# Summing squares in bursts of four tiles, and passing sums of head outputs through DRAM, in a two-layer decoder step

## The chip, the core and the metric

One core of a Trainium2 chip runs the whole program. The metric is the device time of one execution in microseconds, the median of three runs. TensorE (PE) does the matmuls, VectorE (DVE) and ScalarE (ACT) the elementwise work, GpSimd (POOL) a few additions, and SyncE (SP) issues the DMAs, in order.

## The reference, cut to what matters

Two trunk layers run over 512 prompt tokens and 64 sample tokens (8 sequences of 8). In a layer:

```python
h = rmsnorm(x, pre_g)
proj = h @ w_in                                # 2048 -> 6144 columns
u, gp, q, k, v, gr = jnp.split(proj, SPLITS, axis=-1)
pool_y = pool_mixer(u, ...) * silu(gp)         # four groups of 256 channels
ret_y = head_rmsnorm(retention(q, k, v, ...)) * silu(gr)   # four heads of 256 channels
mix = concatenate([pool_y, ret_y]) @ w_out     # 2048 -> 2048
x = x + rmsnorm(mix, post_g)
ple = rmsnorm(p @ w_ple, ple_g)                # per-layer embedding, 256 -> 2048
gate = sigmoid(x @ w_ple_gate + b)
x = x + gate * ple
```

An rmsnorm needs, per token, the sum of the squares of all 2048 channels.

## The kernel before, in words

Activations lie with channels on the 128 partitions and the 576 tokens along the row, in tiles of 128x576 float32. A matmul takes half a row, 288 columns. To keep precision each operand is split into a high and a low part (`split`, L88: ScalarE copies the high part, L90, VectorE subtracts, L91), and a product is three matmuls (L116 to L118, L136, L226).

The large projections `w_in` (first half of its inputs), `w_out` and the gate's first half go through `unit` (L234), a scheme of seven block products in place of eight. It needs, for each pair of activation tiles x1, x2, the blocks themselves and four sums of them: T1 = b12 - b11, T2 = b22 - T1, T3 = b22 - b12, T4 = b21 - T2. `sums_of_blocks` (L186) takes them with four VectorE subtractions (L194 to L197) and splits the results.

A layer runs in this order:

- `in_first` and `in_phase`: the input projection. In `in_phase` the columns of the second half are computed head by head (`head`, L560): q, k, v, retention, state, norm, silu gate. At its end each head multiplies its two output tiles by the gate (L653) and writes them to `m_dram` (L654).
- The pooling groups (`pool_group`, L656), in the order 3, 2, 1, 0. After each group one pair of head outputs is loaded back from `m_dram` into tiles of the tag `x` (L717) and made into operands for the output projection (L711): splits and the four subtractions, into tiles of the tag `part`.
- `out_phase`: the output projection (16 units, L733), with the pooling outputs loaded and made into operands between units (L738). The squares of its results are summed on VectorE into `ssm` (L326), but for the last two tiles (L748). `rsqrt` (L294) then sums over the partitions on TensorE: `token_sums` (L292) multiplies each quarter of a row with a 128x32 matrix of ones, into 32 partitions of an accumulator of the tag `po` (2 buffers). The reciprocal root is some dozen small VectorE instructions (L300 to L306) in one scratch tile of the tag `tmp`, spread back over all partitions by L310 and L311.
- The embedding, L751 to L770: 16 tiles, each of 12 matmuls (L136) into two accumulators of the tag `acc` (4 buffers). ScalarE squares both halves into a tile of the tag `u` (L316) and copies them to a tile of the tag `part` (L768), which goes to DRAM (L770). `token_sums` sums the square into one accumulator over all 16 tiles (L769).
- The gate: the residual is formed (L778, L781) and split, the b12 blocks into tiles of the tag `u` (`plain="u"`, L817), the projection is run, and each tile is gated and added (L789 on).

Nothing orders the engines by hand but a few lines: `after_all` makes an instruction wait for given others, and `order` puts VectorE and ScalarE instructions behind the last one of a unit. All else is set by a planner that walks the program with costs of its own, takes ready instructions by their place in the program, and gives a tile one of its tag's buffers when its first writer is placed. A tag has a fixed number of buffers (L44): `tmp` 4, `part` 4, `x` 4, `u` 6, `g` 2.

Of the kernel before, what the change touches and what calls it, by code (L numbers as in the profile page):

```python
# [10 lines left out]
AF = mybir.ActivationFunctionType  # L11
ALU = mybir.AluOpType
# [3 lines left out]
L = 2  # L16
KT = 16
# [4 lines left out]
HN = NT // 2  # L22
QN = NT // 4
# [10 lines left out]
def half(ap, h):  # L34
    return ap[:, h * HN:(h + 1) * HN]
# [3 lines left out]
def decoder_kernel(ctx: ExitStack, tc: tile.TileContext, a, decay8):  # L39
    nc = tc.nc  # L40
# [5 lines left out]
    def buf(tag, shape=(P, NT), dt=F32):  # L46
        return sb.tile(list(shape), dt, tag=tag, name=tag, bufs=BUFS.get(tag, 1))
# [13 lines left out]
    def tmp():  # L61
        return buf("tmp")

    def load_const(name, shape):
        t = sb.tile(shape, F32, name="c_" + name)
        nc.sync.dma_start(out=t, in_=a[name])
        return t

    ones = sb.tile([P, 32], F32, name="ones")
# [10 lines left out]
    def dram(name, n=KT):  # L80
        return [tc.dram_tile([P, NT], F32, name=f"{name}{i}") for i in range(n)]

    x_dram, m_dram = dram("x"), [dram(f"m{l}") for l in range(L)]
    ple_dram = [dram(f"ple{l}") for l in range(L)]
    gate_dram = [dram(f"gate{l}") for l in range(L)]
    proj_dram = [dram(f"proj{l}", 48) for l in range(L)]

    def split(hi, lo, src, scale=None):  # L88
# [34 lines left out]
    def mix_tile():  # L123
        return ps.tile([P, 512], F32, tag="po", name="po", bufs=2)
# [17 lines left out]
    def operand_set():  # L142
        return {n: [] for n in ("b11", "b12", "t1", "t2", "t3", "t4", "b21", "b22", "src")}

    def order(ops):
        stack = ExitStack()
        for at in ("tail", "tail_act"):
            if at in ops:
                stack.enter_context(tc.issue_after(ops[at].ins))
        return stack  # L150
# [32 lines left out]
            ops["src"].append((x1[j], x2, new[j]))  # L183
        return ops

    def sums_of_blocks(ops, pairs=range(4), tag="u", engines=None):  # L186
        for j in pairs:
            x1, x2, new = ops["src"][j]
            b11, b12 = x1[:, :HN], x1[:, HN:]
            b21, b22 = x2[:, :HN], x2[:, HN:]  # L190
            eng = engines[j] if engines else nc.vector
            t12, t34 = (buf(tag) for _ in range(2))
            with order(ops):
                eng.tensor_tensor(out=t12[:, :HN], in0=b12, in1=b11, op=ALU.subtract)  # L194
                eng.tensor_tensor(out=t12[:, HN:], in0=b22, in1=t12[:, :HN], op=ALU.subtract)
                eng.tensor_tensor(out=t34[:, :HN], in0=b22, in1=b12, op=ALU.subtract)
                last = eng.tensor_tensor(out=t34[:, HN:], in0=b21, in1=t12[:, HN:], op=ALU.subtract)  # L197
            if eng is nc.vector:
                ops["tail"] = last
            for src, n1, n2 in ((t12, "t1", "t2"), (t34, "t3", "t4")):  # L200
                hi, lo = next(new)((P, NT)), next(new)((P, NT))
                split(hi, lo, src)
                ops[n1].append((hi[:, :HN], lo[:, :HN]))
                ops[n2].append((hi[:, HN:], lo[:, HN:]))
        return ops

    def operands(xs, pairs=range(4), ops=None, tag="u", slots=own_slots):
        ops = operand_set() if ops is None else ops
        for j in pairs:
            blocks(xs, [j], ops, slots)  # L210
            sums_of_blocks(ops, [j], tag)
        return ops

    def plain_unit(raw, ops, d0, d1):
# [75 lines left out]
    def token_sums(sums, src, start, stop):  # L290
        for q in range(4):
            nc.tensor.matmul(sums[32 * q:32 * q + 32], ones, src[:, q * QN:(q + 1) * QN], start=start, stop=stop)  # L292

    def rsqrt(out, srcs, n, sums=None):  # L294
        if sums is None:
            sums = mix_tile()[:, :QN]
            for i, src in enumerate(srcs):
                token_sums(sums, src, i == 0, i == len(srcs) - 1)
        v, t, r = (w[:, i * QN:(i + 1) * QN] for w in (tmp(),) for i in range(3))
        nc.vector.tensor_scalar(v, sums, 1.0 / n, EPS, op0=ALU.mult, op1=ALU.add)  # L300
        nc.vector.tensor_scalar(r.bitcast(I32), v.bitcast(I32), 1, None, op0=ALU.logical_shift_right)
        nc.vector.tensor_scalar(r.bitcast(I32), r.bitcast(I32), -1.0, float(0x5F3759DF), op0=ALU.mult, op1=ALU.add)
        for _ in range(3):
            nc.vector.scalar_tensor_tensor(out=t, in0=r, scalar=-0.5, in1=r, op0=ALU.mult, op1=ALU.mult)
            nc.vector.tensor_tensor(out=t, in0=t, in1=v, op=ALU.mult)
            nc.vector.scalar_tensor_tensor(out=r, in0=t, scalar=1.5, in1=r, op0=ALU.add, op1=ALU.mult)  # L306
        for h in range(2):
            rows = mix_tile()[:, :HN]
            for q in (2 * h, 2 * h + 1):
                nc.tensor.matmul(rows[:, (q % 2) * QN:(q % 2 + 1) * QN], pick[:, q], r, start=True, stop=True)  # L310
            nc.scalar.copy(half(out, h), rows)  # L311

    def square(out, src):
        if isinstance(src, list):
            for h in range(2):
                nc.scalar.activation(half(out, h), src[h], AF.Square)  # L316
        else:
            nc.scalar.activation(out, src, AF.Square)

# [11 lines left out]
    def load_tables():  # L331
# [6 lines left out]
        consts["kdec_s"] = load_const("kdec_s", [P, NH, NS])  # L338
        consts["mask_s"] = load_const("mask_s", [P, NH, 64])
        consts["invcnt"] = load_const("invcnt", [P, 4, 16])  # L340

    def after_all(ins, others):
        for other in others:
            tc.add_manual_dep(
                ins.ins, other.ins.name, mybir.DependencyInfo(mybir.DependencyClass.Sync, mybir.DependencyReason.DATA),
                reason="one burst",
            )

    def retention_state(l, h, s0_ring, qrep, kst, vst, po_s):
        for bg in range(2):  # L350
# [28 lines left out]
    pairs = []  # L379
# [89 lines left out]
    def in_phase(l, raws, r2, rB, cos, sin):  # L469
# [90 lines left out]
        def head(h):  # L560
# [3 lines left out]
            q = rotary(8 + h)  # L564
# [8 lines left out]
            k = rotary(12 + h)  # L573
# [33 lines left out]
            o = [rot_ring.tile() for _ in range(2)]  # L607
# [26 lines left out]
            sq, sq2 = tmp(), tmp()  # L634
# [17 lines left out]
            for i, g in enumerate(silu_gates(20 + h)):  # L652
                nc.vector.tensor_tensor(out=o[i], in0=o[i], in1=g, op=ALU.mult)  # L653
                nc.sync.dma_start(out=m_dram[l][8 + 2 * h + i], in_=o[i])  # L654

        def pool_group(g):  # L656
            w = WINDOWS[g]
# [50 lines left out]
        out_ops = operand_set()  # L708
        for j, g in enumerate(groups):
            pool_group(g)  # L710
            operands(mix_loader(l, 8), [j], out_ops, tag="part")  # L711
        return out_ops

    def mix_loader(l, first):
        def xs(k):
            t = buf("x")
            nc.sync.dma_start(out=t, in_=m_dram[l][first + k])  # L717
            return t
        return xs

    def out_phase(l, raws, ops_out):
# [3 lines left out]
        ops = {0: ops_out, 1: operand_set()}  # L725

        def out_step(n, g, p):
            cts = (2 * p, 2 * p + 1)
            fetch(l, raws, keys[n:n + 2])
            if g == 0:  # L730
                for ct in cts:
                    mo[ct] = slot(28 + ct)
            yield from unit(raws.pop(keys[n]), ops[g], mo[cts[0]], mo[cts[1]], g == 0, nc.gpsimd)  # L733
            fetch(l, raws, keys[n + 2:n + 3])
            if g == 0 and 1 <= p < 5:
                j = p - 1
                with order(ops[0]):
                    operands(mix_loader(l, 0), [j], ops[1], tag="d", slots=spare_slots if j < 2 else early_slots)  # L738
            if g:
                for ct in cts:  # L740
                    if ct < KT - 2:
                        square_into(ssm, mo[ct], ct == 0)
# [3 lines left out]
        last = [tmp() for _ in range(2)]  # L746
# [5 lines left out]
        for k in range(2):  # L752
            t = buf("x")
# [2 lines left out]
            split(hi, lo, t)  # L756
            pp.append((hi, lo))
        sums = mix_tile()[:, :QN]
        for c8 in range(2):
            raw = load_weights(a["w_ple"][l, :, c8 * 8:(c8 + 1) * 8].rearrange("p c k n -> p (c k) n"))  # L760
            w = split_weights(raw, 0, 16)
            for c in range(8):
                ct = c8 * 8 + c
                acc = gemm(w[2 * c:2 * c + 2], pp)
                t, sq = buf("part"), buf("u")
                square(sq, acc)
                for i in range(2):
                    nc.scalar.copy(half(t, i), acc[i])  # L768
                token_sums(sums, sq, ct == 0, ct == KT - 1)  # L769
                nc.sync.dma_start(out=ple_dram[l][ct], in_=t)  # L770

        def residual(first):
            def xs(k):
# [67 lines left out]
        x2, g2 = residual(8), []  # L841
# [7 lines left out]
        for p in range(8):  # L849
            raw = raws.pop(("gate2", p))  # L850
            for c in range(2):
                ct = 2 * p + c
                t = buf("part")
# [14 lines left out]
    ops = None  # L868
    for l in range(L):
        state = in_first(l, raws, ops)  # L870
        ops = in_phase(l, raws, *state)
        ops = out_phase(l, raws, ops)
# [93 lines left out]
```

## Time and profile before

| | |
|---|---|
| median of 3 runs | 2209.13 us (2203.75 to 2210.25) |
| profiled execution | 2208.09 us, span 2206.3 us |
| TensorE | busy 2179.7 us (99%) |
| VectorE | busy 1724.1 us (78%) |
| ScalarE | busy 1059.0 us (48%) |
| DMA | 361.98 MB, mean 164 GB/s |
| granted TensorE clock | 0.999 of full speed |

"Busy" is the time in which at least one instruction of the engine ran; matmuls overlap, and their ends are modelled, so for TensorE the distance from one start to the next says more than a duration. Times in rows are microseconds from the start of the span.

### The profile page before, as it was taken

Reading aid. Unit: us, or ns where it says so; the run is one execution under the profiler, and the core shown is the slowest. Engines: PE = TensorE matmul, PEld = TensorE weight load, DVE = VectorE, ACT = ScalarE, POOL = GpSimd, SP = SyncE. Lnnn points to the kernel's source line nnn. Section 1 sums busy time; section 2 is a strip of 40 time slices with the busy share of each in tenths; the row PEclk is TensorE's granted clock in tenths of the full one; section 3 lists DMA queues with packets and bytes.
Section 4 is the critical chain, followed back from the end, with each engine's and each line's share of the span. In section 5 each row is a group of like instructions: output and inputs, shape, how many; then the busy total and the mean of one; then the engine's idle time right before and its main releaser. Section 6 shows DMA issues by size and latency. Waiting matters only on the chain.

```text
span 2206.3 us, 42552 instructions
## 1 busy us (share of the span) xinstructions
PE 2179.7 (99%) x16692; PEld 2138.2 (97%) x16692; DVE 1724.1 (78%) x3186; ACT 1059.0 (48%) x2097; POOL 89.5 (4%) x65
## 2 busy tenths in 40 slices
PE   8999999999999999999999999999999999999998
PEld 8999999999999999899999999999999999998998
DVE  8788766767689998888877786666676899988865
ACT  5465433444334555655455554433343345566532
POOL 2000000000000110000110000000000011100000
PEclk9999999999999999999999999999999999999999
DMA  6454455546453434556644444455554543345554
GB/s 227 146 195 166 155 169 159 174 160 186 152 177 127 136 118 136 196 171 219 201 161 152 166 156 152 161 178 173 159 171 152 171 147 123 112 144 192 175 197 151
DMA packets 138729, 361.98 MB, mean 164 GB/s; under 512 B 14496, under 2 KB 52896, under 8 KB 117664
## 3 DMA queue, kind: packets, MB, share of 16 engines
q1 hardware_dynamic: 138528, 359.26, 49.3%
q8 instruction: 131, 2.15, 0.4%
q14 instruction: 70, 0.57, 0.1%
HBM read 273.17 MB, written 86.04 MB: 163 GB/s over the span
## 4 chain that ended last, share of the span: by engine, by line
PE 87%; DVE 5%; DMA 5%; issue 2%; ACT 1%; SPq 0%; POOL 0%; DVEq 0%; ACTq 0%; POOLq 0%
PE acc L136 32%; PE acc L118 12%; PE acc L117 12%; PE acc L116 12%; PE acc L226 4%; DMA x<-ple 3%; PE pb L116 3%; PE pb L117 3%; PE pb L118 3%; PE po L292 1%; PE po L136 1%; DVE wl L91 1%; DVE x L801 1%; PE po L359 1%; PE pb L375 1%
## 5 line engine op out<-in xcount | busy, mean ns | idle before, releaser
L136 PE MATMUL acc<-m,wh 128*128 128x288 f32 x3584 | 657.0, 297 | 4.0 <-DVE part L484 4.0
L90 ACT CAST wh<-raw 128x512 fp32r<-128x512 f32 x567 | 350.3, 619 | 530.3 <-PE acc L136 288.1
L117 PE MATMUL acc<-m,wh 128*128 128x288 f32 x1944 | 572.3, 295 | 0.0
L116 PE MATMUL acc<-m,wh 128*128 128x288 f32 x1944 | 570.4, 295 | 0.8 <-ACT m L249 0.8
L118 PE MATMUL acc<-m,wl 128*128 128x288 f32 x1944 | 566.3, 295 | 1.2 <-DVE wl L91 1.2
L136 PEld LDWEIGHTS acc<-m,wh 128*128 128x128 f32 x3584 | 534.7, 189 | 11.7 <-issue 8.4
L91 DVE TENSOR_TENSOR wl<-raw,wh 128x512 fp32r<-128x512 f32 x567 | 395.7, 700 | 130.1 <-ACT wh L90 122.7
L136 PE MATMUL acc<-m,wl 128*128 128x288 f32 x1792 | 396.9, 296 | 0.0
L116 PEld LDWEIGHTS acc<-m,wh 128*128 128x128 f32 x1944 | 364.3, 188 | 2.0 <-ACT m L249 1.5
L117 PEld LDWEIGHTS acc<-m,wh 128*128 128x128 f32 x1944 | 364.8, 188 | 0.0
L118 PEld LDWEIGHTS acc<-m,wl 128*128 128x128 f32 x1944 | 362.3, 188 | 2.1 <-DVE wl L91 2.1
L90 ACT CAST wh<-S 128x512 fp32r<-128x512 f32 x356 | 220.6, 620 | 252.8 <-PE acc L117 146.1
L136 PEld LDWEIGHTS acc<-m,wl 128*128 128x128 f32 x1792 | 292.6, 189 | 1.9 <-issue 1.4
L91 DVE TENSOR_TENSOR wl<-S,wh 128x512 fp32r<-128x512 f32 x356 | 250.8, 706 | 24.6 <-ACT wh L90 23.2
L239 POOL TENSOR_TENSOR S<-raw 128x512 f32<-128x512 f32 x45 | 71.4, 1588 | 1923.6 <-DMA raw<-in_w_out 664.9
L484 DVE TENSOR_TENSOR part<-acc,part 128x288 f32<-128x288 f32 x192 | 79.3, 451 | 69.8 <-PE acc L136 67.3
L239 DVE TENSOR_TENSOR S<-raw 128x512 f32<-128x512 f32 x133 | 94.8, 712 | 10.8 <-DMA raw<-in_w_in 7.4
L116 PE MATMUL pb<-m,wh 128*128 128x288 f32 x324 | 95.3, 294 | 0.6 <-ACT wh L90 0.6
L117 PE MATMUL pb<-m,wh 128*128 128x288 f32 x324 | 95.5, 295 | 0.0
L118 PE MATMUL pb<-m,wl 128*128 128x288 f32 x324 | 95.0, 293 | 0.0
L249 ACT COPY d<-acc 128x288 f32<-128x288 f32 x228 | 86.1, 394 | 0.0
L254 DVE TENSOR_TENSOR d<-d,acc 128x288 f32<-128x288 f32 x114 | 51.3, 450 | 39.6 <-PE acc L118 39.3
(264 smaller groups left out, 3289.6 us busy)
## 6 DMA issues: line engine op xcount, KB each, us to landing
raw<-in_w_in SPq DMA_DIRECT2D x95, 1024.0 KB, 5.3
raw<-in_w_out SPq DMA_DIRECT2D x32, 1024.0 KB, 4.8
raw<-in_w_gate SPq DMA_DIRECT2D x32, 1024.0 KB, 5.3
proj<-d SPq DMA_DIRECT2D x96, 288.0 KB, 2.2
part<-proj SPq DMA_DIRECT2D x96, 288.0 KB, 3.0
m<-in_state_ret SPq DMA_DIRECT2D x64, 256.0 KB, 3.3
out_new_ret_s<-m SPq DMA_DIRECT2D x64, 256.0 KB, 3.2
x<-m SPq DMA_DIRECT2D x48, 288.0 KB, 3.4
```

What stands on the lines that cost most here:

```text
L90: nc.scalar.copy(hi, src)
L91: return nc.vector.tensor_tensor(out=lo, in0=src, in1=hi.bitcast(F32), op=ALU.subtract)
L116: nc.tensor.matmul(out, wh, xh, start=start, stop=False, **kw)
L117: nc.tensor.matmul(out, wh, xl, start=False, stop=False, **kw)
L118: nc.tensor.matmul(out, wl, xh, start=False, stop=stop, **kw)
L136: nc.tensor.matmul(acc[h], u, v[:, h * HN:(h + 1) * HN], start=(i == 0 and passno == 0), stop=(i == n - 1 and passno == 2),)
L226: nc.tensor.matmul(acc[h], w[:, j], xs[h][passno == 1], start=(i == 0 and j == 0 and passno == 0), stop=(i == 1 and j == 3 and passno == 2),)
L239: eng.tensor_tensor(out=s, in0=x, in1=y, op=op)
L249: ops["tail_act"] = nc.scalar.copy(dst, src)
L254: return nc.vector.tensor_tensor(out=dst, in0=dst, in1=src, op=ALU.add)
L292: nc.tensor.matmul(sums[32 * q:32 * q + 32], ones, src[:, q * QN:(q + 1) * QN], start=start, stop=stop)
L484: nc.vector.tensor_tensor(out=half(t, h), in0=acc[h], in1=half(t, h), op=ALU.add)
```

## The change

Two edits that have nothing to do with each other:

1. In the embedding the 16 tiles' squares are collected, and after every fourth tile `together` sums four of them with 16 matmul calls in one go. The first of these waits for the last square (`last_square`, `after_all`). The squares are kept in `tmp`, `tmp`, `tmp`, `tmp`, `g`, `g`, `u`, `u`, by turns, instead of `u`.
2. The four subtractions for a pair of head outputs are done at the end of `head`, from the tiles still on chip, into two tiles of the tag `x`; these are written to a new DRAM buffer, `sums_dram`. After a pooling group the pair's operands are made from four loaded tiles instead of two, by splits alone. `ops["tail"]` is not set there any more.

```diff
+    sums_dram = [dram(f"sums{l}", 8) for l in range(L)]
...
+    def block_sums(eng, x1, x2, t12, t34):
+        b11, b12 = x1[:, :HN], x1[:, HN:]
+        b21, b22 = x2[:, :HN], x2[:, HN:]
+        eng.tensor_tensor(out=t12[:, :HN], in0=b12, in1=b11, op=ALU.subtract)
+        eng.tensor_tensor(out=t12[:, HN:], in0=b22, in1=t12[:, :HN], op=ALU.subtract)
+        eng.tensor_tensor(out=t34[:, :HN], in0=b22, in1=b12, op=ALU.subtract)
+        return eng.tensor_tensor(out=t34[:, HN:], in0=b21, in1=t12[:, HN:], op=ALU.subtract)
+
+    def sums_of_blocks(ops, pairs=range(4), tag="u", engines=None, sums=None):
         for j in pairs:
             x1, x2, new = ops["src"][j]
...
+            if sums:
+                t12, t34 = sums(2 * j), sums(2 * j + 1)
+            else:
+                t12, t34 = (buf(tag) for _ in range(2))
+                with order(ops):
+                    last = block_sums(eng, x1, x2, t12, t34)
+                if eng is nc.vector:
+                    ops["tail"] = last
...
+    def together(sums, srcs, start, stop):
+        for i, src in enumerate(srcs):
+            for q in range(4):
+                mm = nc.tensor.matmul(
+                    sums[32 * q:32 * q + 32], ones, src[:, q * QN:(q + 1) * QN],
+                    start=start and i == 0, stop=stop and i == len(srcs) - 1,
+                )
+                if q == i == 0:
+                    after_all(mm, [last_square[0]])
...
             for i, g in enumerate(silu_gates(20 + h)):
                 nc.vector.tensor_tensor(out=o[i], in0=o[i], in1=g, op=ALU.mult)
                 nc.sync.dma_start(out=m_dram[l][8 + 2 * h + i], in_=o[i])
+            sums = [buf("x") for _ in range(2)]
+            block_sums(nc.vector, *o, *sums)
+            for i, t in enumerate(sums):
+                nc.sync.dma_start(out=sums_dram[l][2 * h + i], in_=t)
...
             pool_group(g)
-            operands(mix_loader(l, 8), [j], out_ops, tag="part")
+            operands(loader(m_dram[l][8:]), [j], out_ops, sums=loader(sums_dram[l]))
...
         sums = mix_tile()[:, :QN]
+        squares = []
...
-                t, sq = buf("part"), buf("u")
+                t, sq = buf("part"), buf(("tmp", "tmp", "tmp", "tmp", "g", "g", "u", "u")[ct % 8])
                 square(sq, acc)
                 for i in range(2):
                     nc.scalar.copy(half(t, i), acc[i])
-                token_sums(sums, sq, ct == 0, ct == KT - 1)
                 nc.sync.dma_start(out=ple_dram[l][ct], in_=t)
+                squares.append(sq)
+                if len(squares) == 4:
+                    together(sums, squares, ct == 3, ct == KT - 1)
+                    squares = []
```

## Rows read from the trace of the kernel before

**Rows 1.** The page: span, and busy time of TensorE.

```profile
span 2206.3 us, 42552 instructions
...
PE 2179.7 (99%) x16692; PEld 2138.2 (97%) x16692; DVE 1724.1 (78%) x3186; ACT 1059.0 (48%) x2097; POOL 89.5 (4%) x65
```

**Rows 2.** Waits of TensorE: waiter, releaser, total us, times, longest us.

```profile
PE acc L136 <- DVE part L484: 4.0, 2, 2.0
...
PE acc L118 <- DVE wl L91: 1.2, 3, 0.5
PE po L359 <- DMA u<-in_state_pool: 1.0, 1, 1.0
```

**Rows 3.** Timeline of TensorE, embedding of layer 0: start, us, instructions merged.

```profile
883.67 1.92 PE L292 MATMUL po<-u,ones 128*32 128x144 f32 x56
885.52 0.53 PE L136 MATMUL acc<-d,wh 128*128 128x288 f32 x2
...
887.08 0.29 PE L136 MATMUL acc<-d,wl 128*128 128x288 f32 x1
887.30 0.45 PE L292 MATMUL po<-u,ones 128*32 128x144 f32 x8
887.68 0.53 PE L136 MATMUL acc<-d,wh 128*128 128x288 f32 x2
...
889.25 0.29 PE L136 MATMUL acc<-d,wl 128*128 128x288 f32 x1
889.47 0.44 PE L292 MATMUL po<-u,ones 128*32 128x144 f32 x4
889.84 0.53 PE L136 MATMUL acc<-d,wh 128*128 128x288 f32 x2
...
906.18 0.53 PE L226 MATMUL acc<-m,wh 128*128 128x288 f32 x2
...
912.30 0.44 PE L292 MATMUL po<-u,ones 128*32 128x144 f32 x4
```

**Rows 4.** Timeline of ScalarE, the same stretch.

```profile
866.85 0.41 ACT L316 ACTIVATE u<-acc 128x288 f32<-128x288 f32 x1 [0.87 <-PE acc L136]
...
872.84 1.26 ACT L318 ACTIVATE tmp<-m 128x576 f32<-128x576 f32 x2
...
904.55 0.41 ACT L316 ACTIVATE u<-acc 128x288 f32<-128x288 f32 x1 [0.66 <-PE acc L136]
...
905.14 1.44 ACT L90 CAST u<-m 128x288 fp32r<-128x288 f32 x4
```

**Rows 5.** Timeline of VectorE, the same stretch.

```profile
876.18 0.31 DVE L300 TENSOR_SCALAR tmp<-po 128x144 f32<-128x144 f32 x1 [2.62 <-PE po L292]
...
881.35 0.31 DVE L306 SCALAR_TENSOR_TENSOR tmp<-tmp 128x144 f32<-128x144 f32 x1
...
889.98 2.75 DVE L781 TENSOR_TENSOR m<-m,x 128x576 f32<-128x576 f32 x4
```

**Rows 6.** Busy us by stretch: length, PE, PEld, DVE, ACT, POOL, granted clock, DMA.

```profile
320.00:600.00 280.00, 279.63 (x2206) 270.07 (x2205) 184.63 (x376) 115.19 (x237) 0.00 (x0) 1.00 0.53 168
...
622.00:645.00 23.00, 20.99 (x159) 20.79 (x158) 20.64 (x47) 9.07 (x18) 0.00 (x0) 1.00 0.63 217
...
884.00:907.00 23.00, 23.00 (x214) 17.31 (x207) 19.01 (x31) 19.52 (x56) 0.00 (x0) 1.00 0.80 271
...
1717.00:1740.00 23.00, 20.99 (x147) 20.79 (x146) 19.60 (x45) 7.79 (x16) 0.00 (x0) 0.93 0.62 212
```

**Rows 7.** Timeline of VectorE, pooling stage of layer 0.

```profile
635.30 0.45 DVE L196 TENSOR_TENSOR part<-x 128x288 f32<-128x288 f32 x1
...
639.29 0.81 DVE L484 TENSOR_TENSOR part<-acc,part 128x288 f32<-128x288 f32 x2
```

**Rows 8.** The chain that ended last: start, us, what; pooling stage, layers 0, 1.

```profile
639.88 4.47 PE acc L136 x32
...
1733.98 6.01 PE acc L136 x32
```

More of the change, by code (lines that the diff above doesn't have):

```diff
@@ L184, in blocks @@
         return ops
-    def sums_of_blocks(ops, pairs=range(4), tag="u", engines=None):
+    def block_sums(eng, x1, x2, t12, t34):
[6 more added lines that the diff above has]
+    def sums_of_blocks(ops, pairs=range(4), tag="u", engines=None, sums=None):
         for j in pairs:
             x1, x2, new = ops["src"][j]
-            b11, b12 = x1[:, :HN], x1[:, HN:]
-            b21, b22 = x2[:, :HN], x2[:, HN:]
             eng = engines[j] if engines else nc.vector
[L192 to L199, printed above, removed]
+            if sums:
[6 more added lines that the diff above has]
+                    ops["tail"] = last
             for src, n1, n2 in ((t12, "t1", "t2"), (t34, "t3", "t4")):
@@ L205, in sums_of_blocks, with operands @@
         return ops
-    def operands(xs, pairs=range(4), ops=None, tag="u", slots=own_slots):
+    def operands(xs, pairs=range(4), ops=None, tag="u", slots=own_slots, sums=None):
         ops = operand_set() if ops is None else ops
@@ L210, in operands @@
             blocks(xs, [j], ops, slots)
-            sums_of_blocks(ops, [j], tag)
+            sums_of_blocks(ops, [j], tag, sums=sums)
         return ops
@@ L311, in rsqrt, with after_all @@
             nc.scalar.copy(half(out, h), rows)
+    last_square = [None]
+    def after_all(ins, others):
+        for other in others:
+            tc.add_manual_dep(
+                ins.ins, other.ins.name, mybir.DependencyInfo(mybir.DependencyClass.Sync, mybir.DependencyReason.DATA),
+                reason="one burst",
+            )
     def square(out, src):
@@ L315, in square @@
             for h in range(2):
-                nc.scalar.activation(half(out, h), src[h], AF.Square)
+                last_square[0] = nc.scalar.activation(half(out, h), src[h], AF.Square)
         else:
@@ L340, in load_tables @@
         consts["invcnt"] = load_const("invcnt", [P, 4, 16])
[L342 to L347, printed above, removed]
     def retention_state(l, h, s0_ring, qrep, kst, vst, po_s):
@@ L710, in in_phase, with loader @@
             pool_group(g)
-            operands(mix_loader(l, 8), [j], out_ops, tag="part")
+            operands(loader(m_dram[l][8:]), [j], out_ops, sums=loader(sums_dram[l]))
         return out_ops
-    def mix_loader(l, first):
+    def loader(tiles):
         def xs(k):
             t = buf("x")
-            nc.sync.dma_start(out=t, in_=m_dram[l][first + k])
+            nc.sync.dma_start(out=t, in_=tiles[k])
             return t
@@ L737, in out_step @@
                 with order(ops[0]):
-                    operands(mix_loader(l, 0), [j], ops[1], tag="d", slots=spare_slots if j < 2 else early_slots)
+                    operands(loader(m_dram[l]), [j], ops[1], tag="d", slots=spare_slots if j < 2 else early_slots)
             if g:
```

## Prediction

> **What bounds the kernel now.** I read the page's busy times first, then TensorE's waits, then its timeline instruction by instruction in the two stages that the change touches, then ScalarE's and VectorE's timelines beside it. TensorE is busy for 2179.7 of 2206.3 us [rows 1]: there are 26.6 us of idle time in all, some of it the start of the program. A change can pay only by giving TensorE less to do or by closing one of its few gaps. Its waits are short and few [rows 2]: 4.0 us in two waits for VectorE's addition to a projection tile (L484), one in each layer's pooling stage, 1.2 us in three for split weights, most of it right behind that stage, and 1.0 us for a pool state from DRAM.
>
> The profiled execution took 2208.09 us, 1.8 more than its span and 1.04 less than the median of the runs; the sum below is made against it, and 1.0 is added at the end.
>
> **Part 1: the bursts.** What TensorE pays for summing squares is read from start to start. A stride inside the projection is 0.13 us. Around the run of eight instructions at 887.30 (one tile: four quarters in two passes) the matmuls before and after start at 887.08 and 887.68, so the run costs 0.60 - 0.13 = 0.47 us. Around the run of four at 889.47 (half a tile: the two quarters whose square is ready) it is 889.84 - 889.25 - 0.13 = 0.46 us: half the work, the same price. The 56 instructions at 883.67 (seven tiles) end with the next projection at 885.52: 1.85 us, 0.26 per tile [rows 3]. So a run costs about 0.2 us for going in and out and 0.26 us for each tile in it, and a half tile is no cheaper than a whole one. Layer 0 has one run of 56, one of eight and 16 of four, the last at 912.30, when the next stage has begun; layer 1 has the same. That is 2.0 + 0.47 + 16 x 0.46 = 9.8 us per layer. Four runs of four tiles cost 4 x (0.2 + 4 x 0.26) = 5.0. The change takes 4.8 us of TensorE's time per layer, 9.6 in all, if the planner keeps a burst together.
>
> What it gives back comes from where the squares are kept. Before, all 16 went to `u`, six buffers. Now squares 0 to 3 go to `tmp`, four buffers, which the mixer norm just before it also uses: two squares of the last output tiles (ScalarE, 872.84) and the scratch of its rsqrt (first written at 876.18) [rows 4, 5]. Tiles of one tag seem to be handed out in the order of the program's first writes. The trace shows it: the four casts into `u` for the gate stage had their inputs from 889.98 on [rows 5], ScalarE was not full (19.52 of 23 us) [rows 6], and yet they ran at 905.14, directly behind the square at 904.55 that opens the last `u` of the embedding [rows 4]. By that order square 0 can't be placed before the rsqrt scratch is. Before, the first square ran at 866.85 [rows 4]; it and the next five filled TensorE's time until the rsqrt was through. Now the results of embedding tiles 0 and 1 stay in their accumulators (four buffers, two per tile) until about 873.5 to 875, and TensorE has nothing after the last output product but half a tile. I count by hand: output products end some 0.6 us earlier, since less lies between them, at 871.5; half a projection fills 0.8; then 1.2 idle until the two last squares are taken and summed. From there tiles 2, 3 and 4 follow at 1.6 each (12 matmuls by 0.13). Square 3 needs the fourth `tmp`, the scratch itself, which comes back with the last matmul that spreads the norm over the rows; the rsqrt takes 881.66 - 876.18 = 5.5 us on VectorE [rows 5], so that is near 881. Tile 5 waits for accumulators for some 0.5, and the gaps around them make another 0.5. Together 2.2 us of new idle time per layer; TensorE's share of part 1 is then 4.8 - 2.2 = 2.6 us per layer, 5.2 in all.
>
> The ends of this: nothing given back if the squares find buffers at once (9.6 gained), and a loss if square 0 too has to wait until the rsqrt has returned its scratch (rival 4). I take the hand count, because the order of the `u` casts is the nearest row. ScalarE is the second limit: from 884 to 907 it is busy for 19.52 of 23 us [rows 6], so it can follow a stage that is some 3 us shorter, hardly one that is 5 us shorter. The gate stage's casts still come behind the last square, as now.
>
> **Part 2: the sums of head outputs.** Per head four subtractions of 0.45 us (the L196 row) go from the pooling stage to the head's end, two writes and two reads of 288 KB are added, and the splits of the sums read what is loaded. In the head stage VectorE is busy for 184.6 of 280 us [rows 6] and the subtractions are the last thing that a head does, so I cost them at nothing: TensorE has its next head's projections; uncovered they would be 8 x 4 x 0.4 = 13 us. SyncE's queue gets 16 writes and 16 reads more; what stands behind them are weight fetches and projection loads. The price if these come late is bounded by what a late load costs TensorE now: 1.0 us [rows 2], and 3 if each layer gets one such wait more and the first grows as much.
>
> In the pooling stage TensorE stands for 2 us at 637.9, since the addition that frees its accumulators starts at 639.29 behind a VectorE queue without a break, in which two of the subtractions stand, at 635.30 and right after it [rows 7]. Their starts are 0.37 apart: 0.74 us of the 2 go. Layer 1 has the same order. At the change to the output stage the waits for split weights (0.6 per layer [rows 2]) have the same queue before them; I take 0.4. So 1.1 per layer, between 0 and 2.6. What is late next there is the split of the weight that the addition stands behind. In layer 1 there is more to have: after the same gap of 2 us the 32 matmuls behind it take 6.01 us, against 4.47 in layer 0 [rows 8], and the granted clock of the stretch is 0.93, against 1.00 [rows 6]. That is TensorE at the lower of its levels, 1.2 instead of 2.4 GHz, for a while. If the gap gets shorter, the 1.54 us go; I count 1.0. Part 2: 1.1 + 1.1 + 1.0 = 3.2, between a loss of 3 and a gain of 2.6 + 2.6 + 1.5 = 6.7.
>
> **Sum.** 2208.1 - 5.2 - 3.2 = 2199.7, with 1.0 for the median 2200.7.
>
> **Rivals.**
> 1. Everything is had: no new wait in the embedding stage and all pooling gaps close. 2208.1 - 9.6 - 6.7 + 1.0 = 2192.8. For it: each gap has a VectorE queue before it. Against: the shared `tmp`. Chance 0.08.
> 2. ScalarE or the shared buffers take back nearly all of part 1 and the pooling gaps only move, as the split that follows is late anyway: 3 gained, 2206. For it: 19.52 of 23 us; against: two us of ScalarE's idle time lie just where tile 6 waited. Chance 0.26.
> 3. The change doesn't do what it says: only the first matmul of a burst waits for the last square, so the planner may put projections between the others, and each piece pays its 0.2 again. Part 1 nothing, part 2 as forecast: 2205. Against: all inputs are ready then, and seven tiles already ran in one piece. Chance 0.06.
> 4. Slower: square 0 waits for the rsqrt scratch to come back, not just to be placed. Then tiles 0 and 1 fill the accumulators and TensorE stands from about 874 to 881 and 0.9 more for square 0 and its copies, with 14 projections and 5.0 us of sums left (27.2 us): 909.1. Now the next stage begins at 906.18 with three runs of 0.46 still to come [rows 3], 907.5. So 1.6 is lost per layer; with a fall of the clock after each such gap (1.54) 6.3, and no gain in part 2: 2208.1 + 6.3 + 1.0 = 2215. It decides as soon as no `tmp` is free between 868 and the end of the rsqrt. Chance 0.12.
> 5. The gap of 1.2 us that I expect before the embedding stage is enough to bring the clock down, as the 2 us gap did in one layer of two: 1.54 per layer, 2204. Chance 0.10. The Trainium skill, "TensorE: Matmul & The Clock Gate", section "HAM oscillation — how this bites in real kernels", has it that idle gaps between groups of matmuls put the engine back to the half clock, so that each group starts cold; the trace agrees in layer 1 (0.93) and not in layer 0 (1.00 after the same gap).
>
> The forecast has 0.38, with a range of its own from 2197 to 2204 (2 us of doubt on each part). Leaving out half of rival 1 and most of rival 4, the range is 2192 to 2212. A measurement here tells a difference of 0.3%, 6.6 us, from none: faster is below 2202.5, slower above 2215.8. Faster: 0.29 of the forecast, 0.08 of rival 1, 0.06 of rival 2, 0.03 of rival 5, 0.01 of rival 3, 0.47 in all; slower: 0.05 of rival 4 and 0.03 for mishaps; the rest, 0.45, within.
>
> **What would show it.** Right: four runs of 32 sum matmuls per layer, each 1.2 us from projection to projection; the first embedding square at 873 to 875 instead of 866.85; TensorE idle for 1 to 2.5 us between 871 and 882; the wait for L484 down from 2 to about 1.3, and 32 matmuls behind it at 4.47 in both layers; 16 more writes and reads. Wrong: squares at 867 (rival 1), runs of other lengths (3), an idle stretch of over 5 us (4), a granted clock below 1.00 at 875 to 885 (5), or ScalarE without a pause until 905 (2).

## The result, and the profile after

The changed kernel takes 2196.24 us (median of four runs, 2194.33 to 2199.76), the kernel before, run beside it, 2208.97: a ratio of 0.995, with an interval of 0.9936 to 0.9963, so 8 to 14 us less. The forecast was 2200.7. The sum was right within 5 us; of its two parts one came nearly as worked out, and the other is a larger gain with a loss on top that I had bounded too low.

The profiled execution of the changed kernel took 2199.76 us, the longest of its four; a stage is therefore read from the traces, the total from the medians. The page, against [rows 1]:

```profile
span 2198.0 us, 42624 instructions
...
PE 2168.8 (99%) x16692; PEld 2137.7 (97%) x16692; DVE 1722.3 (78%) x3186; ACT 1058.9 (48%) x2097; POOL 87.4 (4%) x65
```

TensorE has exactly as many matmuls as before and is busy 10.9 us less: the sums became cheaper, not fewer, and some 1.5 us of it are the slow matmuls of layer 1's pooling stage [rows 8], which are gone. Its idle time, 29.2 us by the page, did not shrink but grew by 2.6. What it consists of has changed. TensorE's waits, against [rows 2] (waiter, releaser, total us, times, longest):

```profile
PE po L378 <- DMA m<-in_state_ret: 7.1, 5, 3.3
...
PE acc L137 <- ACT part L792: 2.8, 4, 1.0
PE po L304 <- ACT tmp L342: 2.2, 2, 1.1
```

The 4.0 us for the addition in the pooling stage (now L503) are gone. New are 2.8 and 2.2 us in the embedding, both for ScalarE, and 7.1 us for retention states from DRAM, which were 0.5 us before.

Since both programs have 16692 matmuls, the n-th of one can be set against the n-th of the other. That tells where the time went (after minus before, in us, layer 0 and layer 1):

| stage | layer 0 | layer 1 |
|---|---|---|
| heads, with the late state loads | +3.4 | +1.3 |
| pooling, the gap | -2.1 | -3.7 |
| pooling, the rest, to the output stage | -1.8 | -1.2 |
| output stage | +1.1 | +0.7 |
| embedding | -2.0 | -3.7 |
| gate | +0.7 | -1.4 |

With 0.3 at the start these rows make -8.4, and the spans differ by 8.3. The medians differ by 12.7; where the other 4.4 us lie, no trace shows. Executions of this kernel differ by over 5 us, so a row of under 1 us is no finding.

**The bursts.** TensorE in the embedding of layer 0, against [rows 3]:

```profile
874.69 0.53 PE L137 MATMUL acc<-d,wh 128*128 128x288 f32 x2 [0.95 <-ACT part L792]
...
881.82 1.19 PE L304 MATMUL po<-tmp,ones 128*32 128x144 f32 x32 [1.10 <-ACT tmp L342]
...
890.05 0.29 PE L137 MATMUL acc<-d,wl 128*128 128x288 f32 x1
890.27 0.70 PE L304 MATMUL po<-g,ones 128*32 128x144 f32 x16
890.79 0.67 PE L304 MATMUL po<-u,ones 128*32 128x144 f32 x16
891.39 0.54 PE L137 MATMUL acc<-d,wh 128*128 128x288 f32 x2
...
901.78 0.53 PE L137 MATMUL acc<-d,wh 128*128 128x288 f32 x2 [0.51 <-ACT part L792]
```

Each layer has four runs of 32 and no other (the second and the fourth stand as two rows of 16, since their squares lie in two tags). From the projection before the second run to the one behind it are 891.39 - 890.05 = 1.34 us, 1.21 without the projection's own 0.13. Two gaps stand ahead of the first burst, 0.95 and 1.10 us. ScalarE, against [rows 4], shows why:

```profile
871.98 1.26 ACT L344 ACTIVATE tmp<-m 128x576 f32<-128x576 f32 x2
...
873.65 0.70 ACT L342 ACTIVATE tmp<-acc 128x288 f32<-128x288 f32 x2
...
880.26 0.89 ACT L328 COPY long<-po 128x288 f32<-128x288 f32 x2
881.04 0.72 ACT L342 ACTIVATE tmp<-acc 128x288 f32<-128x288 f32 x2
...
901.33 0.70 ACT L792 COPY part<-acc 128x288 f32<-128x288 f32 x2 [0.82 <-DMA ple<-part]
```

The first embedding square stands at 873.65, behind the two squares of the mixer norm (L344), instead of 866.85. Square 3 stands at 881.04, behind the copies that end the norm. The last row is something else: a copy waits until an earlier `part` has landed in DRAM, and TensorE waits with it (0.51 at 901.78).

**The pooling stage.** VectorE's additions for the tile on which TensorE stood, against [rows 7], with the second long scan of the pooling group (`TENSOR_TENSOR_SCAN`, a running sum along the row). Before, the scan:

```profile
637.57 1.21 DVE L680 TENSOR_TENSOR_SCAN tmp<-d 128x512 f32<-128x512 f32 x1
```

After, the additions and the scan:

```profile
638.13 0.81 DVE L503 TENSOR_TENSOR part<-acc,part 128x288 f32<-128x288 f32 x2
...
639.53 1.21 DVE L703 TENSOR_TENSOR_SCAN tmp<-d 128x512 f32<-128x512 f32 x1
```

Before, the additions (639.29) stood behind this scan; now they go ahead of it. TensorE needs them at 641.26 and finds them done. Busy time by stretch, against [rows 6] (length, PE, PEld, DVE, ACT, POOL, granted clock, DMA share, GB/s):

```profile
622.00:645.00 23.00, 23.00 (x176) 23.00 (x175) 20.96 (x46) 13.02 (x26) 0.00 (x0) 1.00 0.91 310
884.00:907.00 23.00, 21.97 (x202) 20.05 (x202) 16.20 (x28) 19.96 (x57) 0.00 (x0) 1.00 0.84 287
1715.00:1738.00 23.00, 23.00 (x175) 23.00 (x174) 20.91 (x46) 11.39 (x23) 0.00 (x0) 1.00 0.92 313
```

TensorE is busy for all 23 us of both pooling stretches, and the clock of layer 1 is 1.00 instead of 0.93. VectorE is not less busy there (20.96 against 20.64): with the subtractions gone, other work stands in the stretch.

**The state loads.** SyncE's queue in head 3 of layer 0, where the loss is. Before:

```profile
572.42 1.02 SPq L377 DMA_DIRECT2D out_new_ret_s<-m  x2
573.67 0.35 SPq L102 DMA_DIRECT2D raw<-in_w_in  x1
575.37 1.32 SPq L354 DMA_DIRECT2D m<-in_state_ret  x2
```

After:

```profile
573.43 0.42 SPq L103 DMA_DIRECT2D raw<-in_w_in  x1
573.94 0.91 SPq L396 DMA_DIRECT2D out_new_ret_s<-m  x2
583.25 1.07 SPq L373 DMA_DIRECT2D m<-in_state_ret  x2
```

SyncE's wait for these stores from 540 to 600 us, before and after (the same columns as TensorE's waits):

```profile
SPq L354 <- DMA out_new_ret_s<-m: 3.3, 4, 1.3
```

```profile
SPq L373 <- DMA out_new_ret_s<-m: 10.1, 4, 8.3
```

And TensorE after the change, at the first matmuls that need the states:

```profile
587.71 1.07 PE L378 MATMUL po<-m,u 128*32 128x256 f32 x16 [3.28 <-DMA m<-in_state_ret]
```

A load of the next states goes into the buffers that the stores of the last ones read (a ring of four), so it can't start before the stores have landed. Before, the two stores went ahead of a 1 MB weight fetch, and the loads followed 2 us later; now the fetch goes 0.5 us ahead of the stores, the longest wait for a store to land is 8.3 us instead of 1.3, and the loads start at 583.25 instead of 575.37.

### The profile page after: what moved, and what is told of

Its sections match the earlier page's. It is cut to its first block, busy times and chain, and to the rows that moved or that the text cites. A ratio compares the mean times of both kernels' runs of the same rounds, so it can differ in the third digit from the quotient of the medians.

```text
span 2198.0 us, 42624 instructions
## 1 busy us (share of the span) xinstructions
PE 2168.8 (99%) x16692; PEld 2137.7 (97%) x16692; DVE 1722.3 (78%) x3186; ACT 1058.9 (48%) x2097; POOL 87.4 (4%) x65
## 2 busy tenths in 40 slices
DMA packets 143337, 371.42 MB, mean 169 GB/s; under 512 B 15008, under 2 KB 53408, under 8 KB 122272
## 4 chain that ended last, share of the span: by engine, by line
PE 87%; DMA 6%; DVE 4%; ACT 1%; issue 1%; SPq 0%; POOL 0%; ACTq 0%; DVEq 0%; POOLq 0%
PE acc L137 31%; PE acc L117 13%; PE acc L118 13%; PE acc L119 13%; PE acc L233 4%; PE pb L118 3%; PE pb L117 3%; PE pb L119 3%; DMA x<-ple 3%; DMA out_new_ret_s<-m 1%; PE po L137 1%; DVE wl L92 1%; PE po L378 1%; DMA m<-in_state_ret 1%; DVE x L828 1%
## 5 line engine op out<-in xcount | busy, mean ns | idle before, releaser
L92 DVE TENSOR_TENSOR wl<-raw,wh 128x512 fp32r<-128x512 f32 x567 | 404.0, 713 | 126.2 <-ACT wh L91 120.3
L503 DVE TENSOR_TENSOR part<-acc,part 128x288 f32<-128x288 f32 x192 | 79.1, 451 | 73.8 <-PE acc L137 73.0
```

The source lines that it names most:

```text
L92: return nc.vector.tensor_tensor(out=lo, in0=src, in1=hi.bitcast(F32), op=ALU.subtract)
L503: nc.vector.tensor_tensor(out=half(t, h), in0=acc[h], in1=half(t, h), op=ALU.add)
```

## The experiments

Each ran beside the kernel before on the same chip; the profile of each is of one execution. The intervals are for the ratio to the kernel before.

**Part 1 alone.** The embedding as in the change; `head` and the pooling groups as before.

```diff
-            operands(loader(m_dram[l][8:]), [j], out_ops, sums=loader(sums_dram[l]))
+            operands(mix_loader(l, 8), [j], out_ops, tag="part")
```

> Part 1 alone: bursts of four, squares in tmp, g and u; head pairs as before. My theory: the embedding stage gains 5 to 6 us over both layers (four runs of 32 sum matmuls of 1.2 us per layer, less two gaps of about 1 us each behind the late squares), the 2 us wait for the projection addition (L484 of before) stays in each layer: 2203 (2201 to 2205). Rival: the bursts carry the whole gain of 12.7: 2196 to 2197.

Measured: 2199.61 us (2195.81 to 2202.19) against 2208.11, ratio 0.9963 (0.995 to 0.9976): 5 to 11 us faster. That is more than expected (5 to 6 us); the trace shows 6.4 of it, since the matmul count gives -2.7 us in the embedding of layer 0 and -3.7 in that of layer 1. TensorE's waits:

```profile
PE acc L136 <- DVE part L502: 4.0, 2, 2.0
...
PE po L303 <- ACT tmp L341: 2.2, 2, 1.1
...
PE po L377 <- DMA m<-in_state_ret: 1.3, 2, 0.7
```

The two gaps of the embedding belong to part 1 and the pooling gap doesn't. The states cost 1.3 us here, not 7.1; in SyncE's queue the two stores go ahead of the fetch (573.73 against 574.97), as before.

**Part 2 alone.** The sums through DRAM; the embedding as before, each square summed as it comes.

```diff
+                token_sums(sums, sq, ct == 0, ct == KT - 1)
-                squares.append(sq)
-                if len(squares) == 4:
-                    together(sums, squares, ct == 3, ct == KT - 1)
```

> Part 2 alone: sums through DRAM; the embedding sums tile by tile as before. My theory: the 2 us wait in the pooling stage is gone in both layers and with it the slow matmuls of layer 1, while the head stage waits for state loads for some 5 us more than before: 2202 (2200 to 2204), and 9.8 us per layer of sum runs remain. Rival: part 2 gains nothing by itself, 2207 to 2210, and the closed gap comes from a plan that the bursts changed.

Measured: 2203.31 us (2201.85 to 2210.13) against 2208.11, ratio 0.9989 (0.9978 to 1.0): between nothing and 5 us. By the ratios the parts are worth 8.2 and 2.4 us, together 10.6, and the whole change 11.0: within their intervals they add. Its waits:

```profile
PE po L378 <- DMA m<-in_state_ret: 5.9, 4, 3.5
...
PE po L378 <- DMA u<-in_state_pool: 2.2, 1, 2.2
```

No wait for L503 is left in either layer, and the states cost 8.1 us. So the gain and the loss are both of part 2. In layer 1 the longest of these waits also brings the clock down: 16 matmuls that take 1.07 us elsewhere take 1.93 behind it, and the stretch from 1671 to 1690 has a granted clock of 0.82:

```profile
1679.29 1.93 PE L378 MATMUL po<-m,u 128*32 128x256 f32 x16 [3.45 <-DMA m<-in_state_ret]
```

**Which side of part 2 does what.** The kernel before without the subtractions for head outputs, and without their way through DRAM.

```diff
-            t12, t34 = (buf(tag) for _ in range(2))
+            t12, t34 = (x1, x2) if plain else (buf(tag) for _ in range(2))
...
-            operands(mix_loader(l, 8), [j], out_ops, tag="part")
+            operands(mix_loader(l, 8), [j], out_ops, plain=True)
```

> The kernel before with the four subtractions per pair of head outputs left out (the splits take the loaded tiles themselves, so the output projection's results are wrong for these pairs); nothing passes through DRAM. If VectorE's load is what makes the pooling gap, the 2 us wait for L484 falls to 1.3 (only the 0.74 that stands in the queue is taken away) or to nothing (if the order is planned anew), and the state loads of the head stage wait no longer than before (0.5 us). Rival: the gap closes only with loaded sums, since then no subtraction waits for a load: the wait stays at 2 us here. Second rival for the state loads: they wait here too (over 2 us), so the added DMAs aren't their cause.

Measured once: 2202.1 us. The pooling gap is gone in both layers (2.3 and 3.7 us at the same matmuls), though nothing passes through DRAM: the gap hangs on the subtractions in that stage, not on the way through DRAM. Leaving them out also frees their `part` tiles and lifts an order between instructions (`ops["tail"]`), as the change does; whether their time, the tiles or the order counted isn't told apart. The late states are here too, without one added transfer, first on TensorE, then in SyncE's queue:

```profile
585.80 1.07 PE L360 MATMUL po<-m,u 128*32 128x256 f32 x16 [2.25 <-issue]
```

```profile
572.95 0.38 SPq L378 DMA_DIRECT2D out_new_ret_s<-m  x1
573.55 0.34 SPq L102 DMA_DIRECT2D raw<-in_w_in  x1
574.14 0.38 SPq L378 DMA_DIRECT2D out_new_ret_s<-m  x1
```

The profile names no releaser for this wait, but it ends 3.1 us after the last of the loads goes out at 582.69, and such a load lands after 3.2 us in the median. The fetch has come between the two stores. So the added 9.4 MB aren't the cause; a program that is changed in quite another stage is planned with another order in SyncE's queue.

**Two buffers more for the states.** The change with a ring of six instead of four, so that the next loads need not wait for the last stores.

```diff
-        ... s0_ring = ... Ring(24, 4)
+        ... s0_ring = ... Ring(24, 4, (44, 45))
```

> The changed kernel with six buffers in place of four for the retention states in the head stage (two more tiles of on-chip memory). My theory: in the changed kernel the state loads wait for buffers whose stores land late, because a 1 MB weight fetch stands before them in SyncE's queue; with two buffers more two of the four loads of a half need no store to land, so TensorE's wait for state loads falls from 7.1 us to under 2, and the time by 3 to 6 us: 2192 (2190 to 2194). Rival: the loads themselves are slow (DMA engines shared with weights), the wait stays over 5 us: 2196.

Measured: 2192.91 us (2191.97 to 2196.08) against 2206.03, ratio 0.9943 (0.9928 to 0.9958). The time alone doesn't tell it apart from the changed kernel, since the intervals overlap. In its trace TensorE no longer waits for a state's DMA; its waits and SyncE's queue at the place shown above:

```profile
PE acc L234 <- DVE part L826: 2.5, 1, 2.5
...
PE acc L138 <- DVE part L504: 0.2, 1, 0.2
```

```profile
573.27 0.35 SPq L104 DMA_DIRECT2D raw<-in_w_in  x1
573.73 0.97 SPq L374 DMA_DIRECT2D m<-in_state_ret  x2
575.12 1.02 SPq L397 DMA_DIRECT2D out_new_ret_s<-m  x2
```

The loads now go ahead of the stores. At the two places, in layers 0 and 1, the trace gains 3.4 and 2.5 us on the changed kernel, and gives part of it back (2.5 in one wait of the gate stage). It also answers a doubt about the pooling gap: in the changed kernel TensorE comes to it 3.5 us late in layer 0, and might find the addition done for that reason alone. Here it comes on time, and the wait for the addition is 0.2 us in all.

**The stores in another queue.** The change with the state stores issued by GpSimd.

```diff
-                    nc.sync.dma_start(out=a["new_ret_s"]..., in_=s0)
+                    nc.gpsimd.dma_start(out=a["new_ret_s"]..., in_=s0)
```

> The changed kernel with the stores of the sample states issued by GpSimd's queue instead of SyncE's, so that no weight fetch of SyncE's queue stands before them. If the place in the queue makes them late, they land in 3 to 4 us (median of the changed kernel 5.0, longest 9.4), TensorE's wait for state loads falls under 2 us: 3 to 5 us less than the changed kernel. Rival: the DMA engines are shared whatever queue issues, the stores land as late (8 us behind a fetch) and the wait of 7 us stays.

Measured once: 2196.28 us, a span of 2194.5 against 2198.0. TensorE's wait for states falls from 7.1 to 1.0 us, but at the place shown above two loads still stand behind stores. TensorE's wait, GpSimd's stores, and SyncE's loads:

```profile
PE po L378 <- DMA m<-in_state_ret: 1.0, 1, 1.0
```

```profile
574.72 1.46 POOL L396 DMA_DIRECT2D out_new_ret_s<-m  x2 [2.17 <-DVE m L395]
```

```profile
574.48 8.06 SPq L373 DMA_DIRECT2D m<-in_state_ret  x3
```

The stores go out 0.8 us after the fetch (573.93), and the second of the three loads starts at 581.53, 6.8 us after the stores, against 9.3 in the changed kernel and 3.0 before. Over the whole program a store lands after 4.2 us in the median and 7.8 at most, against 5.0 and 9.4. The stores still land late, although they are no longer behind the fetch in its queue; they only no longer hold up TensorE. The place in SyncE's queue is therefore not the whole of why such stores land late.

**Other buffers for the squares.** The change with `u` first and `tmp` last.

```diff
-                ... ("tmp", "tmp", "tmp", "tmp", "g", "g", "u", "u")[ct % 8]
+                ... ("u", "u", "u", "u", "g", "g", "tmp", "tmp")[ct % 8]
```

> The changed kernel with the squares kept in u, u, u, u, g, g, tmp, tmp by turns. My theory: the first square then need not stand behind the norm's scratch; it runs near 867, and the gaps of 0.95 and 1.1 us before the first burst go: 4 us less than the changed kernel, 2192 (2190 to 2194). Rival: ScalarE is the limit and the gaps only move to the second half of the stage: 2196, within 1 us of the changed kernel.

Measured: 2193.26 us (2190.95 to 2200.41) against 2208.11, ratio 0.9941 (0.9921 to 0.996). ScalarE's first squares and TensorE's sums:

```profile
867.23 0.41 ACT L342 ACTIVATE u<-acc 128x288 f32<-128x288 f32 x1
...
888.35 1.19 PE L304 MATMUL po<-u,ones 128*32 128x144 f32 x32
889.35 0.67 PE L304 MATMUL po<-g,ones 128*32 128x144 f32 x16
889.84 0.67 PE L304 MATMUL po<-tmp,ones 128*32 128x144 f32 x16
```

With `tmp` out of the first four, the first square is back at 867.23 and both gaps ahead of the first burst are gone: they came from the shared buffers. The first eight tiles are summed in one run of 64. By its time this isn't told apart from the changed kernel (the intervals overlap), though its span, 2192.9 us, is 5.1 us shorter. One gap of 0.64 us comes later in the stage.

**Bursts of two.** All squares in `u`, summed after every second tile.

```diff
-                if len(squares) == 4:
+                if len(squares) == 2:
```

> The changed kernel with bursts of two tiles and all squares in u, as before. By a price of 0.2 us per run and 0.26 per tile a run of two costs 0.72, eight runs 5.8 us per layer, 0.8 more than four runs of four; the first square runs near 867 again, and the gaps of 0.95 and 1.1 us before the first burst go: embedding stage 1 us per layer shorter than in the changed kernel. Rival: a run's price is in its instructions, so that pairs cost as much as single halves (7 us and more per layer).

Measured once: 2199.78 us, a span of 2198.0, that of the changed kernel. A pair's run costs 0.72 us and the first takes six tiles at once; the embedding of layer 0 gains 4.1 us on the changed kernel, and the gate behind it gives 2.7 back; layer 1 gains 2.0 there and gives back 4.3:

```profile
882.79 1.68 PE L304 MATMUL po<-u,ones 128*32 128x144 f32 x48
886.20 0.70 PE L304 MATMUL po<-u,ones 128*32 128x144 f32 x16
...
934.70 0.40 PE L118 MATMUL acc<-m,wh 128*128 128x288 f32 x1 [1.58 <-DVE m L92]
```

**Both mends.** The change with `u` first and the ring of six.

> Both edits on the changed kernel: squares in u, u, u, u, g, g, tmp, tmp, and six state buffers. If the two gains are of different stages they add: 3 to 5 us of the first and 3 to 6 of the second, 2188 (2185 to 2191). Rival: one gap takes the other's place, 2191 to 2194.

Measured over five rounds: 2189.85 us (2187.95 to 2191.79) against 2206.03, ratio 0.9927 (0.9914 to 0.9939). It is 13 to 19 us below the kernel before. By the medians it is 6.4 below the changed one, but that was not run beside it, and the two intervals just touch. Its profiled execution has a span of 2186.2 us, and this is left of the waits for states:

```profile
PE po L379 <- DMA m<-in_state_ret: 1.1, 1, 1.1
```

## Why the prediction was right, and where it was off

**Price of a burst: right.** Four runs of 32 at about 1.2 us, as worked out from 0.2 per run and 0.26 per tile [rows 3]; a pair's run bears it out (0.2 + 2 x 0.26 = 0.72, measured 0.72). Rival 3 falls: no burst was split. (Its time adds up to 2205.9, not 2205.)

**Give-back in the embedding: right in mechanism and size.** The first square at 873.65 (forecast 873 to 875), square 3 behind the rsqrt's scratch, gaps of 0.95 and 1.10 us; the variant with `u` first takes away exactly these. The trace gives 2.0 and 3.7 us per layer, 5.7 in all, against 5.2. About half of the difference between the layers lies in what I hadn't foreseen, copies that wait for `ple` writes: the waits of 0.34 and 0.51 us in layer 0 have no partner in layer 1. Rival 2 had ScalarE as the limit; it is nearly full (19.96 of 23 us), but TensorE is idle for 1.0 us of that stretch, not 5. Rival 4 needed a stand of over 5 us; none came. Rival 1 had no new wait here; it came true only in the pooling stage.

**The clock: rival 5 falls.** Its granted level is 1.00 in the 12 us around the new gaps, in both layers:

```profile
872.00:884.00 12.00, 9.94 (x108) 8.90 (x108) 8.26 (x19) 9.40 (x27) 0.00 (x0) 1.00 0.47 182
1963.00:1975.00 12.00, 9.94 (x108) 8.91 (x107) 8.20 (x20) 9.59 (x27) 0.00 (x0) 1.00 0.45 175
```

The length of one gap doesn't decide it in these runs: 2.01 us brought the clock down in layer 1 of the kernel before and not in layer 0, 2.25 us at 585.80 did without the subtractions (0.79 from 584 to 592), 2.49 us at 1098.35, in the gate stage, did with the ring of six (0.86 from 1096 to 1108), 3.28 us at 587.71 did not after the change (1.00 from 584 to 592), and 3.45 us at 1679.29 did with part 2 alone. The Trainium skill, "TensorE: Matmul & The Clock Gate", section "HAM oscillation — how this bites in real kernels", tells of a kernel whose waits for DMAs, about 3 to 5 us between groups of matmuls, make every group start cold; of the gaps here that are as long, the one of 3.45 us agrees (0.82) and the one of 3.28 us doesn't (1.00). The falls behind 2.01 to 2.49 us come after shorter gaps than those.

**The pooling gap: the term that was mis-sized.** I gave back 0.74 of 2 us per layer, the time of two subtractions, as if all else in VectorE's queue stayed where it was. Both gaps closed wholly: 4.0 us of waits went where I had 1.5, and with them the 1.5 us of the slow clock (I counted 1.0). But the order did not stay: the additions now go ahead of the scan that stood before them. That the gap hangs on the subtractions, with their tiles and their order, is shown by leaving them out; that TensorE's lateness isn't what closed it, by the ring of six. The 0.4 per layer at the change of stage is at least met (-1.8 and -1.2 from the gap to the output stage), though no run measured it by itself.

**The late loads: the bound was too low.** I allowed 3 us at most, from what a late load cost before. The trace shows 4.7 (3.4 + 1.3), 6.6 more in the waits for `in_state_ret`. I had counted the added DMAs and looked at what stands behind them; the loss came from a fetch and two stores that the change doesn't touch, which the planner put in another order. Two kernels show that the traffic isn't it (without added transfers the wait is there) and that the shared buffer carries it (with two more it goes). What is open: why the planner turned the two round, which was not tried by fixing the order, and how much of the stores' delay is their place behind the fetch, since from another queue the loads still started 6.8 us after them.

**The output stage** lost 1.8 us in the trace of the changed kernel, some of it in waits of a few tenths for splits; I had costed it at nothing. It is within what two executions differ by, and no run was made for it.

So the terms behind the total are: embedding -5.7 (forecast -5.2), the pooling stages with their clock and the change of stage -8.8 (-3.2), state loads +4.7 and output stage +1.8 (0 each). They make -8.0, and -8.4 was forecast: a gain and a loss that I had both set too low stood against each other, and that the sum came so near is luck in its second part. The narrower range that I gave the forecast itself, 2197 to 2204, was missed by 0.8 us.

## What to carry to other kernels

Read the price of going in and out of a kind of matmul from start to start around runs of different lengths: two lengths give the price per run and per tile, and what bundling is worth follows. Where buffers of one tag are handed out in the order of the program, a tile's tag is a place in a queue: give the first tiles of a stage a tag that the stage before doesn't end with. Where a planner orders a queue, a change in one stage can reorder another; after any change look first at loads that go into a buffer which a store still reads, and give them a buffer more.

## What the hardware showed that was not expected

Two stores of 256 KB, issued 0.5 us behind a 1 MB load, let the next load start 9.3 us after them (573.94 to 583.25), where two issued ahead of such a load let it start after 3.0 (572.42 to 575.37). The added 9.4 MB (371.42 against 361.98) show no price of their own: the kernel without them waits for states too (2.3 us for their DMA and 3.0 without a named releaser, against 7.1), and within their intervals the parts add up without one.
